# Turned row tiles of the hybrid layer: whole-row stores and 128-byte block loads for two of three token groups

## The chip, the cores and the metric

The kernel runs on one core of one Trainium2 chip. The metric is the device time of one execution in microseconds, the median over several runs. The engines are named as in the profile: PE is TensorE, DVE is VectorE, ACT is ScalarE, POOL is GpSimd, and SP is SyncE, which only issues DMAs. ScalarE's own DMA queue is shown as ACTq, SyncE's as SPq.

## The reference, cut to what matters

One layer for 2048 prompt rows and 128 sample rows of width 1024 (17 tiles of 128 rows). The first half mixes tokens (a gated delta rule in four heads beside a short gated convolution), and ends in the projection `w_o`. The change touches what comes then:

```python
mix = jnp.concatenate([o, sc_out.astype(x.dtype)], axis=-1) @ w_o
x = x + rmsnorm(mix, norm_mix_post)

h = rmsnorm(x, norm_ffn_pre)
f = (jax.nn.silu(h @ w_gate) * (h @ w_up)) @ w_down
x = x + rmsnorm(f, norm_ffn_post)
```

`w_gate` and `w_up` are 1024 x 2816, `w_down` is 2816 x 1024, all in float32.

## The kernel before, in words

**Stages.** Five groups of row tiles go through the mixing stage. Then the output stage takes the 17 row tiles one after the other (`o_tile`), and gate and up work on three token groups (`FGROUPS`) of tiles 0 to 5, 6 to 11 and 12 to 16. For each group 22 blocks `f` of 128 feed-forward columns are computed, each with seven products of a Strassen-like scheme (`product`, line 1436, 12 matmuls each since every factor is split into a high and a low part). The down projection follows.

**One output tile.** `o_load` brings the tile's mixed rows (`mr`, one buffer, two DMAs) and its rows of x (`xo`, two buffers). `mix_split` makes the high part `mh` on ScalarE (line 1154) and the low part `ml` on VectorE (line 1155). 48 matmuls (line 1198) fill two PSUM banks. ScalarE squares them (line 1202), VectorE scales them and adds them to `xo` (lines 1207 and 1208), ScalarE's queue stores the sum (`x2d`, line 1209). `o_rows` then makes the input of gate and up: squares on ScalarE (line 1217), a power on GpSimd, a scaling `hx` (line 1221) and a turn `ht` on VectorE (line 1223), which transposes each 32x32 block in place. `ht` has one buffer, so the turn of the next tile waits until the stores of this one have read it.

**The turned tile in DRAM.** Gate and up need columns of features on partitions, that is, the whole transpose. The 32x32 blocks are turned inside, and DMAs put them in their places. Before the change the store does that: `hTd` of a group is `[1024, rows of the group]`, and four DMAs a tile on SP's queue (line 1227) write 32 partitions each in runs of 32 floats, 128 bytes. `ffn_load` (line 1315) then reads eight tiles `fh` of 128 features in whole rows. ScalarE multiplies them by the gain (`ffn_gain`, line 1320), VectorE makes sums of them (`ffn_sums`), and `ffn_prep` splits them for the products.

**Order.** The first seven output tiles run alone. The eighth (`O_SPLIT`) and the next six have the preparation of token group one woven between them, and blocks 0 of gate and up begin among the last tiles. Weights of group one are loaded (`rg`, `ru`, lines 1399 and 1400), cast and split on ScalarE, VectorE and GpSimd into `fw` (lines 1411 and 1412), and some of the split weights are stored (`fsplit`, line 1414), which groups two and three load again (line 1409). Twelve slots hold split weights, a block uses seven. While group one is in gate and up, group two's `fh` tiles are loaded, one a block from f = 4, and multiplied and summed; the same for group three during group two. The instructions of every engine, and the DMAs of a queue, run in the order in which a planner at build time has put them: it simulates the engines with its own costs and takes, of the instructions that are ready, the one that comes first in the program. `tc.issue_after(x)` holds an instruction behind x on x's engine.

Of the kernel before, what the change touches and what calls it, by code (L numbers as in the profile page):

```python
# [9 lines left out]
F32 = mybir.dt.float32  # L10
# [7 lines left out]
P = 128  # L18
# [79 lines left out]
def kernel(  # L98
# [30 lines left out]
    mixo = [dram.tile([P, H, P], F32, name=f"mixo{t}") for t in range(NT)]  # L129
    mixs = [dram.tile([P, 4, len(g) * P], F32, name=f"mixs{gi}") for gi, g in enumerate(GROUPS)]  # L130
    wsplit = [dram.tile([P, 2, KD, P], F32, name=f"wsplit{j}") for j in range(28)]
    hTd = [dram.tile([D, len(g) * P], F32, name=f"hTd{gi}") for gi, g in enumerate(FGROUPS)]
    partd = [[dram.tile([len(g) // 2, P, 7, len(c) // 2, P], F32, name=f"partd{gi}_{ch}") for ch, c in enumerate(FCHUNKS)]
             for gi, g in enumerate(FGROUPS)]
    lastd = [dram.tile([P, 2, len(c) // 2, P], F32, name=f"lastd{ch}") for ch, c in enumerate(FCHUNKS)]
# [30 lines left out]
    with ExitStack() as ph:  # L166
# [1005 lines left out]
        def o_load(t):  # L1172
            mr = None
            if t:
                m = oa.tile([P, KD, P], F32, tag="mr", name="mr") if t > 1 else spare[2]
                mr = m[:, 0:4], m[:, 4:8]
                nc.sync.dma_start(out=mr[0], in_=mixo[t])
                gi, i = PLACE[t]
                nc.sync.dma_start(out=mr[1], in_=mixs[gi][:, :, i * P:(i + 1) * P])
            xt = op.tile([P, D], F32, tag="xo", name="xo", bufs=2)  # L1180
            nc.sync.dma_start(out=xt, in_=x[t])
            return mr, xt

        rows_in, omark = {0: o_load(0)}, {}

        def o_tile(t):
            mr, xt = rows_in.pop(t)
            halves_m = [mix_split(mr[kh]) if t else ready_m[kh] for kh in range(2)]
            if t + 1 < NT:
                rows_in[t + 1] = o_load(t + 1)  # L1190
            pss = [psd.tile([P, 512], F32, tag="d", name="dbank"), pft.tile([P, 512], F32, tag="t", name="ftbank")]
            for kh in range(2):
                mh, ml = halves_m[kh]
                for j in range(4):
                    k = 4 * kh + j
                    for ci, (m_, w_) in enumerate(((mh, woh), (mh, wol), (ml, woh))):
                        for n in range(2):
                            T.matmul(pss[n], m_[:, j, :], w_[k][:, n * 512:(n + 1) * 512],
                                     start=(k == 0 and ci == 0), stop=(k == KD - 1 and ci == 2))
            ss = op.tile([P, 4], F32, tag="oss", name="oss", bufs=2)  # L1200
            for n in range(2):
                A.activation(ojunk, pss[n], AF.Square, accum_out=ss[:, n:n + 1])
            V.tensor_add(ss[:, 0:1], ss[:, 0:1], ss[:, 1:2])
            r = rstd(op, ss[:, 0:1], 1, 1.0 / D, EPS, "ox")
            for n in range(2):
                c = slice(n * 512, (n + 1) * 512)
                V.scalar_tensor_tensor(pss[n], pss[n], r, gpost[:, c], op0=ALU.mult, op1=ALU.mult)
                omark["V"] = V.tensor_add(xt[:, c], xt[:, c], pss[n])  # L1208
            nc.scalar.dma_start(out=x2d[t], in_=xt)
            if t + 1 < NT:  # L1210
                o_rows(t, xt, ss)
            else:
                omark["last"] = lambda: o_rows(t, xt, ss)

        def o_rows(t, xt, ss):
            for n in range(2):
                omark["A"] = A.activation(ojunk, xt[:, n * 512:(n + 1) * 512], AF.Square, accum_out=ss[:, 2 + n:3 + n])
            V.tensor_add(ss[:, 2:3], ss[:, 2:3], ss[:, 3:4])
            r = rstd(op, ss[:, 2:3], 1, 1.0 / D, EPS, "oy")
            hx = op.tile([P, D], F32, tag="hx", name="hx") if t else spare[0]  # L1220
            V.tensor_scalar_mul(hx, xt, r)
            ht = op.tile([P, D], F32, tag="ht", name="ht") if t else spare[1]
            V.transpose(ht, hx)
            gi, i = FPLACE[t]
            for b in range(4):
                c = i * P + 32 * b
                nc.sync.dma_start(out=hTd[gi][:, c:c + 32].rearrange("(j f) c -> f j c", f=32),  # L1227
                                    in_=ht[32 * b:32 * b + 32].rearrange("f (j c) -> f j c", c=32))
# [12 lines left out]

    dring, dprep, cast, wl = {}, [], [], []
    SUMS = ("sA", "sB", "sC", "sD")
    SUMF = range(12, 20, 2)

    def down_chunk(ch):
        c = len(FCHUNKS[ch]) // 2
# [59 lines left out]
    with ExitStack() as ph:  # L1307
        ks = ctx.enter_context(tc.tile_pool(name="ks", bufs=1, reuse_waits="tile"))
        fp = ph.enter_context(tc.tile_pool(name="fp", bufs=1, reuse_waits="tile"))

        def ffn_load(gi, fs):
            hw = len(FGROUPS[gi]) * P // 2
            for k in range(KD):
                h = fs.tile([P, 2 * HW], F32, tag="h", name="fh", bufs=KD)
                nc.sync.dma_start(out=h[:, :2 * hw], in_=hTd[gi][k * P:(k + 1) * P])
                yield h[:, :2 * hw]

        def ffn_gain(hs, ks):
            for k in ks:
# [41 lines left out]
                yield X  # L1361

        with tc.tile_pool(name="fs", bufs=1, reuse_waits="tile") as fs:
            hload = ffn_load(0, fs)
            hs = [next(hload) for _ in range(KH)]
            o_tile(O_SPLIT)
            hs += hload
            prep = ffn_prep(0, hs, fs=fs)
            for i in range(len(PARTS)):
                with tc.issue_after(omark["A"].ins), tc.issue_after(omark["V"].ins):  # L1370
                    if i < 2:
                        ffn_gain(hs, range(KH * i, KH * i + KH))
                    hid = next(prep)
                if i + 1 < len(PARTS):
                    o_tile(O_SPLIT + 1 + i)
        fe = ph.enter_context(tc.tile_pool(name="fe", bufs=1, reuse_waits="tile"))

        nw = [0]
# [142 lines left out]
        for gi in range(len(FGROUPS)):  # L1521
            if gi:
                *_, hid = ffn_prep(gi, hs, t3)
            for f in range(NF):
                gate_up(gi, f, hid, gu_start(gi, f, hid))
                if (gi, f) == (0, 0):
                    omark["last"]()
                    ps_o.close()
                    fd = side.enter_context(tc.tile_pool(name="fd", bufs=1, reuse_waits="tile", side="right"))
                if f == 3 and gi + 1 < len(FGROUPS):  # L1530
                    hload, hs = ffn_load(gi + 1, fd), []
                if gi + 1 < len(FGROUPS):
                    if 5 <= f < 5 + KD:
                        with tc.issue_after(gmark["A"].ins):
                            ffn_gain(hs, [f - 5])
                    if 4 <= f < 4 + KD:
                        with tc.issue_after(wl[0].ins):
                            hs.append(next(hload))
                    if f in SUMF:
                        with tc.issue_after(gmark["V"].ins):  # L1540
                            t3 = ffn_sums(gi + 1, hs, fd, t3 if f > SUMF[0] else None, [SUMF.index(f)])
                elif f == 2:
                    side.close()
                    dr = late.enter_context(tc.tile_pool(name="dr", bufs=1, reuse_waits="tile", side="right"))
                    c = len(FCHUNKS[0]) // 2
                    a = dr.tile([P, 2, c * P], F32, tag="ar0", name="ar0")
                    with tc.issue_after(wl[0].ins):
                        nc.sync.dma_start(out=a, in_=partd[0][0][0, :, 0:2].rearrange("p i q c -> p i (q c)"))
                    first_parts = [dr.tile([P, 2, c * P], F32R, name=f"as0{i}") for i in range(3)]
                elif f == 4:  # L1550
                    with tc.issue_after(gmark["A"].ins), tc.issue_after(gmark["V"].ins):
                        for i, b in enumerate(first_parts[:2]):
                            A.copy(b[:, 0], a[:, i])
                            V.tensor_sub(b[:, 1], a[:, i], b[:, 0].bitcast(F32))
                    a = dr.tile([P, 2, c * P], F32, tag="ar0", name="ar0")
                    with tc.issue_after(wl[0].ins):
                        nc.sync.dma_start(out=a[:, 0], in_=partd[0][0][1, :, 0].rearrange("p q c -> p (q c)"))
                    dprep += [down_chunk(ch) for ch in dorder]
                    prep_step(1)
                elif f == 7:  # L1560
                    with tc.issue_after(gmark["A"].ins), tc.issue_after(gmark["V"].ins):
                        b = first_parts[2]
                        A.copy(b[:, 0], a[:, 0])
                        V.tensor_sub(b[:, 1], a[:, 0], b[:, 0].bitcast(F32))
                    prep_step(1)
                elif 10 <= f < 12 + NDR:
                    with tc.issue_after(gmark["A"].ins), tc.issue_after(gmark["V"].ins):
                        prep_step(1)
# [341 lines left out]
```

## Time and profile before

| | |
|---|---|
| time, median of 3 runs | 2432.32 us (2431.96 to 2433.75) |
| time of the profiled execution | 2432.03 us |
| its span | 2430.1 us |
| granted TensorE clock, mean | 0.998 |
| TensorE busy | 2406.1 us (99%) |
| VectorE, ScalarE, GpSimd busy | 1610.4, 1065.5, 560.5 us |
| output tiles and gate and up | from about 850 to 1967 us |
| DMA packets | 317464, of which 95700 under 512 bytes |

The span is the profiled execution from its first to its last instruction. A row of a timeline has the start, the duration, the engine and line, and in brackets the idle time before it with what ended it. A row of stretches has the busy time in each, the number of instructions, the granted clock (1.00 is full speed), the mean busy share of the 16 DMA engines and the GB/s they moved.

### The profile page before, as it was taken

Reading aid. Unit: us, or ns where it says so; the run is one execution under the profiler, and the core shown is the slowest. Engines: PE = TensorE matmul, PEld = TensorE weight load, DVE = VectorE, ACT = ScalarE, POOL = GpSimd, SP = SyncE. Lnnn points to the kernel's source line nnn. Section 1 sums busy time; section 2 is a strip of 40 time slices with the busy share of each in tenths; the row PEclk is TensorE's granted clock in tenths of the full one; section 3 lists DMA queues with packets and bytes.
Section 4 is the critical chain, followed back from the end, with each engine's and each line's share of the span. In section 5 each row is a group of like instructions: output and inputs, shape, how many; then the busy total and the mean of one; then the engine's idle time right before and its main releaser. Section 6 shows DMA issues by size and latency. Waiting matters only on the chain.

```text
span 2430.1 us, 39106 instructions
## 1 busy us (share of the span) xinstructions
PE 2406.1 (99%) x14222; PEld 2207.8 (91%) x14222; DVE 1610.4 (66%) x3042; ACT 1065.5 (44%) x2367; POOL 560.5 (23%) x667
## 2 busy tenths in 40 slices
PE   9999999999999999989999999999999999999998
PEld 7888889999999987889999999999999988888887
DVE  7875755746667465788888844456556555676787
ACT  6645545546444444444443423334333345333443
POOL 1211000001110000155665200000000035455663
PEclk9999999999999999999999999999999999999999
DMA  8774555666776677699877888878998844334376
GB/s 294 251 244 168 220 204 191 251 218 233 269 258 248 226 186 215 168 311 326 302 274 255 288 263 266 257 244 271 303 300 284 262 152 122 108 121 127 112 243 202
DMA packets 317464, 561.37 MB, mean 231 GB/s; under 512 B 95700, under 2 KB 198296, under 8 KB 299992
## 3 DMA queue, kind: packets, MB, share of 16 engines
q1 hardware_dynamic: 218848, 496.42, 61.7%
q10 hardware_dynamic: 98200, 61.41, 8.2%
q8 instruction: 112, 1.84, 0.3%
q0 software_dynamic: 224, 1.05, 0.1%
q14 instruction: 80, 0.66, 0.1%
HBM read 400.09 MB, written 158.70 MB: 230 GB/s over the span
## 4 chain that ended last, share of the span: by engine, by line
PE 51%; DMA 2%; DVE 2%; POOL 1%; issue 1%; SPq 1%; ACT 1%; ACTq 0%; POOLq 0%; DVEq 0%
PE fbank L1436 34%; PE fbank L1626 17%; DMA fsplit<-fw 1%; DMA partd<-pt 1%; SPq L1227 1%; POOL dw L1280 0%; DVE fw L1412 0%; DMA mr<-mixo 0%; DMA ru<-in_w_gu 0%; POOL as L1609 0%; DMA hTd<-ht 0%; ACTq L1473 0%; ACT as L1606 0%; DMA ar<-partd 0%; DMA xo<-in_x 0%
## 5 line engine op out<-in xcount | busy, mean ns | idle before, releaser
L1436 PE MATMUL fbank<-xh,fw 128*128 128x384 f32 (+1 forms) x3696 | 899.1, 326 | 8.4 <-DVE xo L1208 4.0
L1436 PEld LDWEIGHTS fbank<-xh,fw 128*128 128x128 f32 x3696 | 652.2, 188 | 10.8 <-ACT m L1469 3.9
L326 PE MATMUL dbank<-hi,w 128*128 128x384 f32 (+1 forms) x2224 | 650.6, 363 | 0.0
L1436 PE MATMUL fbank<-xl,fw 128*128 128x384 f32 (+1 forms) x1848 | 602.6, 326 | 0.0
L326 PEld LDWEIGHTS dbank<-hi,w 128*128 128x128 f32 x2224 | 409.7, 188 | 40.2 <-issue 3.6
L1626 PE MATMUL fbank<-dw,as 128*128 128x512 f32 x1785 | 415.9, 391 | 1.8 <-DVE as L1609 0.9
L1626 PEld LDWEIGHTS fbank<-dw,as 128*128 128x128 f32 x1785 | 334.6, 188 | 76.0 <-DVE as L1609 1.4
L326 PE MATMUL dbank<-lo,w 128*128 128x384 f32 (+1 forms) x1112 | 396.5, 357 | 0.0
L1436 PEld LDWEIGHTS fbank<-xl,fw 128*128 128x128 f32 x1848 | 347.3, 188 | 0.0
L326 PEld LDWEIGHTS dbank<-lo,w 128*128 128x128 f32 x1112 | 209.3, 188 | 15.7 <-DVE lo L241 0.4
L1609 POOL TENSOR_TENSOR as<-ar,as 128x256 fp32r<-128x256 f32 (+1 forms) x202 | 174.8, 874 | 182.3 <-ACT as L1606 176.7
L1606 ACT CAST as<-ar 128x256 fp32r<-128x256 f32 (+1 forms) x287 | 119.2, 427 | 206.5 <-PE fbank L1626 162.9
L1579 DVE TENSOR_TENSOR acc<-acc,fbank 128x512 f32<-128x512 f32 x219 | 148.1, 683 | 88.2 <-PE fbank L1626 70.8
L1280 POOL TENSOR_TENSOR dw<-dr,dw 128x512 fp32r<-128x512 f32 x48 | 67.8, 1422 | 512.5 <-ACT dw L1278 512.1
L1411 ACT CAST fw<-rg 128x512 fp32r<-128x512 f32 x124 | 77.2, 622 | 233.4 <-PE fbank L1436 140.3
L330 DVE SCALAR_TENSOR_TENSOR acc<-R,vec,acc 128x512 f32<-128x512 f32 (+2 forms) x180 | 120.9, 673 | 27.3 <-ACT acc L367 21.0
L1484 DVE TENSOR_TENSOR c<-u,fbank 128x384 f32<-128x384 f32 (+1 forms) x66 | 34.9, 528 | 94.4 <-PE fbank L1436 94.4
L1480 DVE TENSOR_TENSOR m<-m,m 128x384 f32<-128x384 f32 (+1 forms) x44 | 23.1, 526 | 83.1 <-ACT m L1470 82.9
L1412 POOL TENSOR_TENSOR fw<-rg,fw 128x512 fp32r<-128x512 f32 x44 | 65.5, 1489 | 35.9 <-ACT fw L1411 35.5
L1482 ACT ACTIVATE m<-fbank 128x384 f32<-128x384 f32 (+1 forms) x66 | 31.2, 473 | 90.9 <-PE fbank L1436 75.4
L359 POOL COPY hist<-R 128x3 f32<-128x3 f32 x60 | 18.3, 305 | 217.4 <-ACT R L335 171.9
L1487 ACT ACTIVATE c<-c 128x384 f32<-128x384 f32 (+1 forms) x66 | 33.4, 506 | 79.6 <-DVE c L1486 76.8
(402 smaller groups left out, 3566.6 us busy)
## 6 DMA issues: line engine op xcount, KB each, us to landing
w<-wsplit SPq DMA_DIRECT2D x105, 1024.0 KB, 5.0
fw<-fsplit SPq DMA_DIRECT2D x188, 512.0 KB, 4.7
fsplit<-fw SPq DMA_DIRECT2D x94, 512.0 KB, 4.0
partd<-pt ACTq DMA_DIRECT2D x86, 384.0 KB, 6.2
rg<-in_w_gu SPq DMA_DIRECT2D x62, 512.0 KB, 4.1
wsplit<-w SPq DMA_DIRECT2D x28, 1024.0 KB, 5.0
ar<-partd SPq DMA_DIRECT2D x43, 384.0 KB, 3.1
wr<-in_w_in SPq DMA_DIRECT2D x32, 512.0 KB, 6.5
```

What stands on the lines that cost most here:

```text
L326: T.matmul(ps[:, :c], l[:, k, :], r[k][:, :c], start=(k == 0 and r is hi and l is wh), stop=(k == KD - 1 and l is wl))
L330: r = V.scalar_tensor_tensor(acc, raw(d), w[:, d:d + 1], acc, op0=ALU.mult, op1=ALU.add)
L1280: e.tensor_tensor(out=w[1], in0=v, in1=w[0].bitcast(F32), op=ALU.subtract)
L1411: A.copy(w[:, 0], v)
L1412: e.tensor_tensor(out=w[:, 1], in0=v, in1=w[:, 0].bitcast(F32), op=ALU.subtract)
L1436: T.matmul(ps, w_[:, c], b_[k][:, :hw], start=(first and k == 0 and ci == 0), stop=(k == KH - 1 and ci == 2), skip_group_check=not first)
L1484: V.tensor_add(c21, u2, b3)
L1487: gmark["A"] = A.activation(c12, c12, AF.Silu)
L1579: mark_d["V"] = V.tensor_tensor(out=dst if out is None else out, in0=dst, in1=ps, op=ALU.add)
L1606: ins = mark_d["A"] = A.copy(a[:, 0, :n], v)
L1609: mark_d["V" if e is V else "G"] = e.tensor_tensor(out=a[:, 1, :n], in0=v, in1=a[:, 0, :n].bitcast(F32), op=ALU.subtract)
L1626: ins = T.matmul(ps, a[:, x_, q * P:(q + 1) * P], w[y_], start=(start and q == 0 and ci == 0), stop=(q == c - 1 and ci == 2), skip_group_c ...
```

## The change

Token group one stays as it was in DRAM. For groups two and three (tiles 6 to 16), `hTd` becomes `[4 x tiles, 32, 1024]`, and a turned tile is stored as it stands, one DMA of 128 whole rows of 4096 bytes, on ScalarE's queue. Placing the blocks moves to the load: each `fh` tile is filled by four DMAs on SP's queue, each of 32 partitions, which read runs of 128 bytes (24 runs a partition for group two, 20 for group three). There are 32 such loads a group, two a block from f = 4 to 15 and four in blocks 16 and 17 (`LOADF`), in the order of feature tiles 0, 4, 1, 5, 2, 6, 3, 7; a gain follows in the block after its tile's last load. The sums move from blocks 12, 14, 16, 18 to 12, 14, 17, 19 (`SUMF`). The eight loads of group one go into `o_tile` of tiles 7 and 8, four each, behind the row loads of the next tile.

```diff
-    hTd = [dram.tile([D, len(g) * P], F32, name=f"hTd{gi}") for gi, g in enumerate(FGROUPS)]
+    hTd = [dram.tile([4 * len(g), 32, D] if gi else [D, len(g) * P], F32, name=f"hTd{gi}") for gi, g in enumerate(FGROUPS)]
...
-        def o_tile(t):
+        def o_tile(t, loads=()):
...
             if t + 1 < NT:
                 rows_in[t + 1] = o_load(t + 1)
+            for load in loads:
+                load()
...
-            for b in range(4):
+            if gi:
+                nc.scalar.dma_start(out=hTd[gi][4 * i:4 * i + 4].rearrange("b f c -> (b f) c"), in_=ht)
+            for b in range(0 if gi else 4):
                 c = i * P + 32 * b
                 nc.sync.dma_start(out=hTd[gi][:, c:c + 32].rearrange("(j f) c -> f j c", f=32),
                                     in_=ht[32 * b:32 * b + 32].rearrange("f (j c) -> f j c", c=32))
...
-    SUMF = range(12, 20, 2)
+    SUMF = (12, 14, 17, 19)
+    LOADF = [4 + i // 2 for i in range(24)] + [16 + i // 4 for i in range(8)]
...
+        def ffn_tile(gi, fs):
+            return fs.tile([P, 2 * HW], F32, tag="h", name="fh", bufs=KD)[:, :len(FGROUPS[gi]) * P]
+
-        def ffn_load(gi, fs):
-            hw = len(FGROUPS[gi]) * P // 2
-            for k in range(KD):
-                h = fs.tile([P, 2 * HW], F32, tag="h", name="fh", bufs=KD)
-                nc.sync.dma_start(out=h[:, :2 * hw], in_=hTd[gi][k * P:(k + 1) * P])
-                yield h[:, :2 * hw]
+        def ffn_load(gi, fs, hs):
+            for k in (k for q in range(KH) for k in (q, KH + q)):
+                hs[k] = ffn_tile(gi, fs)
+                for q in range(4):
+                    c = k * P + 32 * q
+                    with tc.issue_after(wl[0].ins):
+                        nc.sync.dma_start(out=hs[k][32 * q:32 * q + 32].rearrange("f (b c) -> f b c", c=32),
+                                          in_=hTd[gi][:, :, c:c + 32].rearrange("b f c -> f b c"))
+                    yield k if q == 3 else None
...
-            hload = ffn_load(0, fs)
-            hs = [next(hload) for _ in range(KH)]
-            o_tile(O_SPLIT)
-            hs += hload
+            hs = [ffn_tile(0, fs) for k in range(KD)]
+            loads = [lambda k=k: nc.sync.dma_start(out=hs[k], in_=hTd[0][k * P:(k + 1) * P]) for k in range(KD)]
+            o_tile(O_SPLIT, loads[:KH])
...
-                    o_tile(O_SPLIT + 1 + i)
+                    o_tile(O_SPLIT + 1 + i, () if i else loads[KH:])
...
-                if f == 3 and gi + 1 < len(FGROUPS):
-                    hload, hs = ffn_load(gi + 1, fd), []
+                if f == 0 and gi + 1 < len(FGROUPS):
+                    hs = {}
+                    hload, loaded = ffn_load(gi + 1, fd, hs), []
                 if gi + 1 < len(FGROUPS):
-                    if 5 <= f < 5 + KD:
-                        with tc.issue_after(gmark["A"].ins):
-                            ffn_gain(hs, [f - 5])
-                    if 4 <= f < 4 + KD:
-                        with tc.issue_after(wl[0].ins):
-                            hs.append(next(hload))
+                    with tc.issue_after(gmark["A"].ins):
+                        while loaded:
+                            ffn_gain(hs, [loaded.pop()])
+                    for _ in range(LOADF.count(f)):
+                        k = next(hload)
+                        loaded += [] if k is None else [k]
```

## The prediction

> **What bounds the kernel now.** I read the page first, then TensorE's waits, then its busy time by stretches, then the timelines around each hole. From the page:
>
> ```profile
> span 2430.1 us, 39106 instructions
> PE 2406.1 (99%) x14222; PEld 2207.8 (91%) x14222; DVE 1610.4 (66%) x3042; ACT 1065.5 (44%) x2367; POOL 560.5 (23%) x667
> L1436 PE MATMUL fbank<-xh,fw 128*128 128x384 f32 (+1 forms) x3696 | 899.1, 326 | 8.4 <-DVE xo L1208 4.0 <-ACT m L1469 3.1 <-ACT m L1470 0.7
> ```
>
> TensorE is busy for all but 24 us, so the change can only win back holes in TensorE, and the slow clock behind a hole. It removes no matmul. Two places in reach of the change have holes: one before 960 us, and the start of gate and up from 1040 us, where line 1436 idles 8.4 us in all. Stretches of 10 us (busy time, matmuls, granted clock, DMA share, GB/s), then three longer ones over that start:
>
> ```profile
> 950.00:960.00 10.00, 7.33 (x26) 0.83 0.65 129
> ...
> 980.00:990.00 10.00, 10.00 (x46) 1.00 0.71 158
> ...
> 1050.00:1060.00 10.00, 9.65 (x46) 0.83 0.99 238
> ```
> ```profile
> 1040.00:1068.00 28.00, 23.66 (x119) 0.94 1.01 300
> 1068.00:1090.00 22.00, 19.29 (x110) 1.00 1.00 340
> 1090.00:1136.00 46.00, 44.81 (x257) 1.00 0.99 352
> ```
>
> The first hole costs more than its idle time. 26 matmuls ran where an undisturbed stretch runs 46, so (46-26)/46 x 10 = 4.3 us are lost: 2.67 idle, the rest at the lower clock. The second place loses 96 - 87.76 = 8.2 us of idle time and (1-0.83) x 10 = 1.7 us of clock, 9.9 together, and the DMA engines are saturated throughout. So 4.3 + 9.9 = 14.2 us is the most that lies here.
>
> **The first hole** is a wait for the store that the change moves. Start, duration, and the idle time before it with what ended it, on SP's queue, ScalarE, VectorE and TensorE:
>
> ```profile
> 933.87 4.77 SPq L1315 DMA_DIRECT2D fh<-hTd  x8
> ...
> 941.72 6.24 SPq L1227 DMA_DIRECT2D hTd<-ht  x4
> ```
> ```profile
> 949.99 1.12 ACT L1154 CAST mh<-mr 128x512 fp32r<-128x512 f32 x2
> ```
> ```profile
> 937.24 1.25 DVE L1223 STREAM_TRANSPOSE ht<-hx 128x1024 f32<-128x1024 f32 x1
> ...
> 947.88 0.75 DVE L1221 TENSOR_SCALAR hx<-xo,oyr 128x1024 f32<-128x1024 f32 x1 [0.73 <-POOL oyr L155]
> 952.64 1.25 DVE L1223 STREAM_TRANSPOSE ht<-hx 128x1024 f32<-128x1024 f32 x1 [4.00 <-DMA hTd<-ht]
> 953.80 1.25 DVE L1155 TENSOR_TENSOR ml<-mr,mh 128x512 fp32r<-128x512 f32 x2
> ```
> ```profile
> 954.51 0.79 PE L1198 MATMUL dbank<-woh,ml 128*128 128x512 f32 x1 [2.67 <-DVE ml L1155]
> ```
>
> Tile 6 is turned by 938.5, but SP is busy with eight loads and with the next tile's rows, and starts the four stores at 941.72. There is one buffer ht, so the turn of tile 7, whose input was ready at 948.6, waits until 952.64. Behind it on VectorE stands ml, for which TensorE waits.
>
> **Part 1, eleven turned tiles (6 to 16) stored in whole rows on ScalarE's queue.** Removed are 44 DMAs on SP, added 11 on ScalarE. Prices: two short stretches, the first filled with the old stores and the second with loads in long rows; then issue times (minimum/median/maximum, ns), and from the page an issue with its us to landing:
>
> ```profile
> 897.60:899.80 2.20, 2.20 (x11) 1.00 1.11 171
> 938.00:940.00 2.00, 2.00 (x10) 1.00 1.02 410
> ```
> ```profile
> L1227 SPq DMA_DIRECT2D hTd<-ht x68: 303/564/3530, 873.3 to 1082.4; - x68
> ...
> L1209 ACTq DMA_DIRECT2D x2d<-xo x17: 326/327/333, 869.1 to 1062.9; - x17
> ```
> ```profile
> x2d<-xo ACTq DMA_DIRECT2D x17, 512.0 KB, 2.6
> ```
>
> The x2d store has the size, shape and queue of the new one: 0.33 us to issue, 2.6 to land. Tile 6 would be issued at about 938.6 and landed by 942, six us ahead of tile 7's input. The turn then runs 948.6 to 949.9, ml can start when the first mh is done (950.6) and ends near 951.3; TensorE ran dry at 951.8. The hole closes, by half a microsecond: **-4.3 us**.
>
> The Trainium skill, "DMA: Bandwidth & Descriptors", section Issuing engines are not separate DMA queues, says that another issuing engine saves only the sequencer's issue time, usually small beside the transfer. By that alone this move would be worth next to nothing and the time would stay at 2432. The first half fits the trace; the second doesn't, since SP's issues took 6.24 us for one tile, and they stood behind others.
>
> **Where it lies in the tail.** The last tiles' stores meet weight loads, split-weight stores and saturated engines; the last row below is the packets from 1040 to 1100 us:
>
> ```profile
> 1045.11 6.15 SPq L1227 DMA_DIRECT2D hTd<-ht  x4
> 1051.36 1.49 SPq L1399 DMA_DIRECT2D rg<-in_w_gu  x1
> ...
> 1075.49 8.29 SPq L1227 DMA_DIRECT2D hTd<-ht  x4
> ```
> ```profile
> 1054.52 1.25 DVE L1223 STREAM_TRANSPOSE ht<-hx 128x1024 f32<-128x1024 f32 x1 [3.07 <-DMA hTd<-ht]
> ```
> ```profile
> 1056.33 0.62 ACT L1411 CAST fw<-rg 128x512 fp32r<-128x512 f32 x1 [3.52 <-DMA rg<-in_w_gu]
> ```
> ```profile
> 1048.60 0.41 PE L1436 MATMUL fbank<-xh,fw 128*128 128x384 f32 x1 [3.37 <-DVE xo L1208]
> ```
> ```profile
> DMA packets 19267, 19.39 MB, mean 323 GB/s; under 512 B 14080, under 2 KB 15083, under 8 KB 19264
> ```
>
> These issues leave SP, so rg and ru go out earlier. A tile's 524,288 bytes take 3.1 us at 171 GB/s and 1.3 at 410: 1.8 us of the engines freed a tile, and at 4096 short packets a tile the 14080 are 3.4 tiles: some 6 us freed in a stretch that is full. Of the 8.4 us idle on line 1436, 4.0 are two waits for xo. The 3.37 at 1048.60 falls before the 3.07 wait for ht and hangs on VectorE's order; I leave it and its 1.7 us of clock where they are. The other, 0.6, comes behind the 3.07 wait and goes. The remaining 4.4 are ScalarE's copies and casts, late through weights and slots held by transfers; I take three quarters, 3.3, since six freed microseconds exceed them but queueing is not additive. Bounds: nothing, or all 9.9. Taken: **-3.9 us**.
>
> **The new wait.** ScalarE now waits for VectorE's turn of each tile; the squares, mh casts, weight casts and copies out of PSUM stand behind it, and TensorE waits for those. In the steady part ScalarE has idle time there:
>
> ```profile
> ACT mh L1154 <- PE ftbank L1198: 19.8, 5, 4.0
> ```
>
> Tile 6's turn ends at 938.5 and that idle time spans it, so the issue and the wait cost nothing; without this cover it would be up to 4 us a tile before TensorE's next mh. In the tail the place in ScalarE's queue isn't visible from the trace of before. Bounds: 0, and 3.4 tiles, rounded up to four, x (1.25 for the turn + 0.33), about 6 us, less what it idles anyway (it waits 3.52 us for rg alone). I take 0, since ScalarE is the idle one there.
>
> **Part 2, loads of groups two and three.** 16 loads of whole rows become 64, each on 32 partitions in runs of 128 bytes: 768 runs (group two) or 640. Nothing in the trace reads runs of 128 bytes from DRAM. The nearest row below is the long-row rate, 410 GB/s (98,304 bytes: 0.24 us), the nearest above the old stores at 171 (0.57 us, or 12 ns a run on each engine), of equal run and partition count but the other way. I take the latter. Reads may be dearer; that end is a rival. Where they run, two a block f, four at f = 16 and 17:
>
> ```profile
> 1218.50:1246.00 27.50, 27.50 (x161) 27.50 (x160) 23.16 (x29) 13.60 (x26) 16.15 (x12) 1.00 0.78 263
> ...
> 1466.00:1493.50 27.50, 27.50 (x160) 27.50 (x159) 12.27 (x23) 8.40 (x17) 0.00 (x0) 1.00 0.87 282
> ```
> ```profile
> SPq L1409 <- PE fbank L1436: 141.9, 66, 3.6
> ```
>
> A block is 84 matmuls, 84 x 27.5/160 = 14.4 us. Two loads are 1.15 us of the engines where one load of 393,216 bytes took 0.96, so the DMA share of 0.78 to 0.87 rises by about 0.01, and TensorE has no hole there. SP spends 64 x 0.56 = 36 us on issues instead of the 44 removed; it waits 141.9 us for TensorE to free weight slots in the 300 us from 1390 on (the last row), which covers them. Cost: **0**. The work of the gains and of the sums is the same; they move by a block or two and end at f = 19 instead of 18, three blocks before their use.
>
> The Trainium skill, same page, section Why small descriptors are slow, gives about 3 cycles of overhead a packet: 128 bytes are 4 beats, so 4/7 of the page's 435 GB/s, an estimate of 249, 0.39 us a load. The store row is slower; with the page's rate the sum stays as it is.
>
> **Part 3, group one's eight loads behind the next tile's rows.** Same bytes. At 933.87 all eight went ahead of the next tile's row loads. Behind them, the rows can come earlier and the gains later, by at most half of those 4.77 us of issues. The first hole was closed above with the old order, so I take 0, with 2.4 us either way.
>
> **Sum.** The profiled execution took 2432.03 us, 0.3 under the median of 2432.32. 2432.0 - 4.3 - 3.9 = 2423.8; I forecast **2424**.
>
> **Rivals.**
> - *Only the first hole closes.* VectorE's order and the weight supply, not the stores, make the tail. For: the largest hole, 3.37 us, is before any wait for ht. Against: rg stands behind 6.15 us of store issues. 2432.0 - 4.3 = 2427.7.
> - *Everything closes*, since xo comes earlier too once row loads aren't late: 2432.0 - 14.2 = 2418. Against: that wait runs through VectorE, whose work there stays.
> - *ScalarE held in the tail* takes the place of the waits removed: -4.3, tail unchanged, + 6 = 2434. It decides if copies out of PSUM stand behind a turn that VectorE does late.
> - *Dear short reads: slower.* Place: group two, where group three's tiles are loaded. Room in a block is 0.13 x 14.4 = 1.9 us plus 0.8 of the old load (327,680 bytes), 2.7 in all, 1.35 a load, 40 runs on each engine: from 34 ns a run on, weights come late. At 40 ns a load takes 1.6: 0.5 us over in 12 blocks and 3.7 in two, 13 us, so 2424 + 13 = 2437, and beyond with a higher price. Against: 34 ns is nearly three times the store's 12.
> - *The change does less than it says*, because the planner that orders the queues shifts other work: 2432.
>
> **How the numbers follow.** A measurement of this kernel can tell about 0.2%, 4.9 us, from no change: faster is under 2427.5, slower over 2437.2. Forecast 0.40, everything 0.14, first hole alone 0.18 (half of it on each side of 2427.5), ScalarE held 0.12, less than it says 0.05, dear reads 0.11. Faster: 0.40 + 0.14 + 0.09 = 0.63. Slower: dear reads and 0.02 of ScalarE held, 0.13. Same: 0.24. The range leaves out most of the dear reads and the edges: 2416 to 2435; the forecast's own is 2420 to 2428.
>
> **What would show it.** Right: no idle time on VectorE's turn for hTd; TensorE full from 950 to 960 at clock 1.00; no store issue of turned tiles on SP after 930; under 8.2 us idle on line 1436; gate and up without a hole from 1140 to 1960, at a DMA share within a few hundredths; new loads issued in under 1 us and landing in 3 to 6. Wrong: holes of TensorE behind fw between 1150 and 1690 (dear reads), or ScalarE idle until ht with TensorE waiting for its copies.

## The result, and the profile after

The changed kernel takes 2420.8 us (median of six, 2419.26 to 2423.34), the kernel before 2433.29 beside it (2431.96 to 2437.0): a ratio of 0.9948, 95% interval 0.9935 to 0.9961. It is faster, by 12.5 us by the medians. The profiled execution took 2421.49 us, its span is 10.6 us shorter than before's (2430.1 to 2419.5).

From the page of the changed kernel, where lines from 1198 on have moved down by two (1200 is the former 1198) and those of gate and up by ten (1446 is the former 1436, 1479 the former 1469); in the experiments they move by a few more:

```profile
span 2419.5 us, 39078 instructions
PE 2402.4 (99%) x14222; PEld 2204.9 (91%) x14222; DVE 1603.4 (66%) x3042; ACT 1064.3 (44%) x2367; POOL 561.3 (23%) x667
L1446 PE MATMUL fbank<-xh,fw 128*128 128x384 f32 (+1 forms) x3696 | 898.2, 326 | 2.7 <-ACT m L1479 1.7
```

TensorE's idle time fell from 24.0 us (2430.1 - 2406.1) to 17.1 (2419.5 - 2402.4), that is by 6.9; its busy time fell by 3.7, with the same matmuls, mostly because the two stretches of 10 us at a granted clock of 0.83 are gone (1.7 us each). Together 10.6, the difference of the two profiled spans; the 12.5 above are between medians of other executions, and a later measurement gives 10.5 (below). The two places, by TensorE's busy time, first in the kernel before (the line of 1040 to 1136 was summed in the prediction), then after (columns: busy us, matmuls, granted clock, DMA share, GB/s):

```profile
1040.00:1136.00 96.00, 87.76 (x482) 0.98 1.00 334
```
```profile
950.00:960.00 10.00, 10.00 (x45) 1.00 0.62 197
1040.00:1136.00 96.00, 94.29 (x543) 1.00 0.93 324
```

The first hole is closed. The start of gate and up has 1.7 us of idle time left of 8.2, and none of the lower clock.

The turned tiles' stores and the new loads in the changed kernel (issue time minimum/median/maximum in ns, first and last start, and, last line, from issue to landing of the loads), and two rows of ScalarE and its queue:

```profile
L1228 ACTq DMA_DIRECT2D hTd<-ht x11: 326/326/327, 942.2 to 1061.9; - x11
```
```profile
L1325 SPq DMA_DIRECT2D fh<-hTd x64: 422/498/3179, 1081.1 to 1617.9; - x64
...
DMA to landing us min/median/max: 4.1/4.6/9.2
```
```profile
942.20 0.33 ACTq L1228 DMA_DIRECT2D hTd<-ht  x1
```
```profile
942.63 0.60 ACT L1204 ACTIVATE ojunk<-dbank 128x512 bf16<-128x512 f32 x1 [6.79 <-DMA fh<-hTd]
```

A store takes 0.33 us to issue, as forecast. But tile 6's left at 942.20, not at 938.6, and ScalarE stood 6.79 us before its next piece of work. TensorE didn't notice. The move to another queue didn't bring this store forward: before it left at 941.72, with short runs on ScalarE's queue (first experiment) at 941.48, with whole rows on SP's at 941.86. What ScalarE stood for, when the turn was done at about 939.0, isn't settled: the profile names the landing of group one's loads.

**Where the time came from** shows in ScalarE's rows of the output tiles. Before, the first mh casts of tiles 15 and 16 and the first squares of tiles 13 to 16:

```profile
1017.14 0.62 ACT L1154 CAST mh<-mr 128x512 fp32r<-128x512 f32 x1 [3.43 <-DMA mr<-mixo]
1018.08 0.59 ACT L1202 ACTIVATE ojunk<-dbank 128x512 bf16<-128x512 f32 x1
...
1030.94 0.62 ACT L1154 CAST mh<-mr 128x512 fp32r<-128x512 f32 x1 [2.89 <-DMA mr<-mixo]
1031.47 0.59 ACT L1202 ACTIVATE ojunk<-dbank 128x512 bf16<-128x512 f32 x1
...
1040.13 0.59 ACT L1202 ACTIVATE ojunk<-dbank 128x512 bf16<-128x512 f32 x1
...
1049.62 0.60 ACT L1202 ACTIVATE ojunk<-dbank 128x512 bf16<-128x512 f32 x1
```

And after:

```profile
1011.27 0.62 ACT L1154 CAST mh<-mr 128x512 fp32r<-128x512 f32 x1 [2.90 <-PE ftbank L1200]
...
1022.24 0.62 ACT L1154 CAST mh<-mr 128x512 fp32r<-128x512 f32 x1 [2.86 <-PE ftbank L1200]
1027.96 0.60 ACT L1204 ACTIVATE ojunk<-dbank 128x512 bf16<-128x512 f32 x1 [0.39 <-PE dbank L1200]
...
1038.94 0.60 ACT L1204 ACTIVATE ojunk<-dbank 128x512 bf16<-128x512 f32 x1 [2.00 <-PE dbank L1200]
```

Before, ScalarE waits for the rows of the next tile (mr), and the squares of tiles 13 and 14, which TensorE has already finished, stand behind that cast. Tile 15's squares (1040.13) stand behind casts of the first split weights instead. VectorE's rows, first before and then after, show the sum that these casts wait for and tile 15's xo, for which TensorE waited 3.37 us:

```profile
1037.77 1.19 DVE L1402 TENSOR_TENSOR sC<-rg,ru 128x512 f32<-128x512 f32 x1 [0.17 <-DMA ru<-in_w_gu]
...
1047.18 0.68 DVE L1208 TENSOR_TENSOR xo<-xo,dbank 128x512 f32<-128x512 f32 x1
```
```profile
1025.63 0.69 DVE L1412 TENSOR_TENSOR sC<-rg,ru 128x512 f32<-128x512 f32 x1 [0.67 <-DMA ru<-in_w_gu]
...
1034.54 0.68 DVE L1210 TENSOR_TENSOR xo<-xo,dbank 128x512 f32<-128x512 f32 x1
```

After, ScalarE's casts and squares above wait for TensorE. The last tile's squares start 10.7 us earlier (1049.62 to 1038.94), tile 15's xo 12.6. SP's queue says where the rows and the weights were held, before and after:

```profile
1021.33 3.59 SPq L1227 DMA_DIRECT2D hTd<-ht  x4
1025.03 0.60 SPq L1177 DMA_DIRECT2D mr<-mixo  x1
...
1031.69 0.38 SPq L1399 DMA_DIRECT2D rg<-in_w_gu  x1
```
```profile
1013.61 0.32 SPq L1177 DMA_DIRECT2D mr<-mixo  x1
...
1019.07 0.33 SPq L1409 DMA_DIRECT2D rg<-in_w_gu  x1
```

The store of one tile holds SP for 3.59 us and the next rows go out right behind it. After the change the last rows (of tile 16) go out 11.4 us earlier, the first gate weights 12.6. That is a loop: late rows, late squares, late xo and turn, late store, and so the next late rows. Whether SP's issue time drives it, or the time of the short runs on the DMA engines, is what the experiments ask.

### The profile page after: what moved, and what is told of

Its sections match the earlier page's. It is cut to its first block, busy times and chain, and to the rows that moved or that the text cites. A ratio compares the mean times of both kernels' runs of the same rounds, so it can differ in the third digit from the quotient of the medians.

```text
span 2419.5 us, 39078 instructions
## 1 busy us (share of the span) xinstructions
PE 2402.4 (99%) x14222; PEld 2204.9 (91%) x14222; DVE 1603.4 (66%) x3042; ACT 1064.3 (44%) x2367; POOL 561.3 (23%) x667
## 4 chain that ended last, share of the span: by engine, by line
PE 93%; DVE 3%; ACT 1%; DMA 1%; POOL 1%; issue 1%; POOLq 0%; SPq 0%; DVEq 0%; ACTq 0%
PE fbank L1446 36%; PE dbank L326 25%; PE fbank L1637 17%; PE dbank L1200 4%; PE ftbank L1200 4%; PE tbank L384 1%; PE gbank L597 1%; PE gbank L604 1%; PE obank L776 1%; PE gbank L768 1%; PE gbank L790 1%; PE obank L798 1%; PE gbank L784 1%; DVE sA L1413 0%; PE gbank L701 0%
```

## The experiments

**The queue alone.** The kernel before, with the four short-run stores of tiles 6 to 16 on ScalarE's queue.

```diff
-                nc.sync.dma_start(out=hTd[gi][:, c:c + 32]...
+                (nc.scalar if gi else nc.sync).dma_start(out=hTd[gi][:, c:c + 32]...
```

> The kernel before with one edit: the four block stores of tiles 6 to 16 are issued on ScalarE's queue instead of SyncE's; layout, runs of 128 bytes and loads stay old. Theory Q (what counts is that the stores leave SyncE's queue, where they stood behind loads and held weight loads up): the wait of the turn for the store before tile 7 goes, the hole near 955 us closes (-4.3 us), and part of the tail's 9.9 us goes too, less what ScalarE now loses by issuing four stores a tile among its copies: ratio to before 0.9955 to 0.9980. Theory L (what counts is the short runs): the first hole closes, the tail stays full of short packets and ScalarE is held by slow issues: 0.998 to 1.003.

Measured: 2441.14 us, ratio 1.0036 (1.0023 to 1.0048): slower. ScalarE and its queue:

```profile
941.48 6.86 ACTq L1227 DMA_DIRECT2D hTd<-ht  x4
```
```profile
948.44 0.60 ACT L1202 ACTIVATE ojunk<-dbank 128x512 bf16<-128x512 f32 x1 [13.00 <-DMA hTd<-ht]
...
1057.14 7.21 ACTq L1227 DMA_DIRECT2D hTd<-ht  x4
1064.39 0.48 ACT L1469 COPY m<-fbank 128x384 f32<-128x384 f32 x1 [7.21 <-DMA hTd<-ht]
```

The four issues hold ScalarE as long as they held SP (6.24 us before), and its squares stand behind them, at the end of 13 us in which ScalarE does no work. The first hole stays (7.56 us busy from 950 to 960), although both theories had it closed, and the tail is worse (84.90 us busy from 1040 to 1136, where it was 87.76): TensorE waits 3.78 us for the copy in the last row. The queue doesn't make an issue cheaper here; it only chooses who is held.

**The layout alone.** The changed kernel with the whole-row stores back on SP's queue.

```diff
-                nc.scalar.dma_start(out=hTd[gi][4 * i:4 * i + 4]..., in_=ht)
+                nc.sync.dma_start(out=hTd[gi][4 * i:4 * i + 4]..., in_=ht)
```

> The changed kernel with one edit: the whole-row store of a turned tile is issued on SyncE's queue. Theory L (one store of long rows instead of four of short runs is what counts): the issue takes about 0.4 us instead of 2.6 to 8.3 a tile, the buffer of the turn comes free in time, and the time is within 2 us of the changed kernel: ratio to before 0.994 to 0.996. Theory Q (the queue counts): the store stands behind group one's loads and the row loads again, the hole near 955 us is back: 0.997 to 0.999.

Measured: 2419.63 us, ratio 0.9945 (0.9932 to 0.9959): the whole gain without ScalarE's queue. Later this kernel ran beside the changed one on one chip:

> The changed kernel once more, beside the next run on one chip, to compare the two queues directly. If ScalarE's queue for the whole-row stores were worth something of its own (ScalarE held by a store costs, or SP relieved by it gains): the two ratios lie apart by 0.002 or more. If, as the runs so far suggest, only the length of the rows counts: both at 0.994 to 0.996 and within 0.001 of each other.

> The changed kernel with the whole-row stores on SP's queue instead of ScalarE's (e2 once more, beside the run above). ScalarE's queue matters: apart from the run above by 0.002 or more. Only the length of the rows matters: 0.994 to 0.996, within 0.001 of it.

Measured: the changed kernel 2421.29 us (2420.56 to 2423.22), ratio 0.9961 (0.9949 to 0.9974); with the stores on SP 2419.22 us (2418.04 to 2420.24), ratio 0.9951 (0.9938 to 0.9965). They lie 0.001 apart, at the border of the second expectation, and the single times don't overlap: SP's queue is some 2 us better, if anything. It is the fastest kernel of this study. Two rows of ScalarE in it show that the stand of 6.79 us is gone:

```profile
939.46 0.60 ACT L1204 ACTIVATE ojunk<-dbank 128x512 bf16<-128x512 f32 x1 [4.29 <-PE dbank L1200]
944.11 0.62 ACT L1154 CAST mh<-mr 128x512 fp32r<-128x512 f32 x1 [3.25 <-DMA mr<-mixo]
```

**Group one's order alone.** The kernel before, with its eight loads of group one behind the next tile's rows (Part 3).

```diff
-            hload = ffn_load(0, fs)
-            hs = [next(hload) for _ in range(KH)]
-            o_tile(O_SPLIT)
-            hs += hload
+            o_tile(O_SPLIT, loads[:KH])
```

> The kernel before with one edit: only the eight loads of group one are moved behind the next tiles' row loads; stores and loads of groups two and three stay old. Prediction: nothing, within 2.4 us: ratio 0.999 to 1.001. Rival O (the order of these loads closes the first hole, since the row loads and the stores of tile 6 no longer stand behind eight loads): 0.998 or less, the hole near 955 us gone.

Measured: 2434.87 us, ratio 1.0008 (1.0000 to 1.0017). TensorE's stretches:

```profile
950.00:960.00 10.00, 10.00 (x46) 1.00 0.97 200
1040.00:1136.00 96.00, 84.41 (x461) 0.96 0.96 314
```

The first hole is closed, with the short stores still on SP and VectorE still waiting 7.0 us for them. It is worth nothing: the tail loses 96 - 84.41 = 11.6 us of idle time and 3.8 of clock where it lost 8.2 and 1.7, so 5.5 us are given back.

**Group one's order undone.** The changed kernel with those loads where they were.

> The changed kernel with one edit: the eight loads of group one go back to their old places. Prediction: as the changed kernel, ratio to before 0.994 to 0.996. Rival O: the first hole comes back, 0.9965 or more.

Measured: 2422.64 us, ratio 0.9959 (0.9946 to 0.9971), about 1.8 us over the changed kernel, inside both intervals. The two orders can't be told apart by the time. Half of the first hole's idle time is back, none of its lower clock, and the tail is that of the changed kernel (94.29 us busy from 1040 to 1136), so the gain there doesn't need the order:

```profile
950.00:960.00 10.00, 8.68 (x39) 1.00 0.57 199
```

**SP's issue time or the DMA engines' time.** Two kernels made from the one with whole rows on SP: each tile stored three times, and each tile stored in sixteen pieces.

```diff
                 nc.sync.dma_start(out=hTd[gi][4 * i:4 * i + 4]..., in_=ht)
+                for n in range(2):
+                    nc.sync.dma_start(out=spareh[2 * t + n], in_=ht)
```
```diff
-                nc.sync.dma_start(out=hTd[gi][4 * i:4 * i + 4]..., in_=ht)
+                for n in range(0, P, 8):
+                    nc.sync.dma_start(out=rows[n:n + 8], in_=ht[n:n + 8])
```

> The kernel with whole rows stored from SP's queue (e2), but each of the eleven turned tiles is stored three times, the second and third time into spare DRAM. Three long-row stores put about 3 x 1.28 = 3.8 us a tile on the DMA engines (1.28 us: 524,288 bytes at 410 GB/s), more than the 3.07 us of the old short-run store (at 171 GB/s), but hold SP for only three issues of some 0.33 us, 1.0 us a tile, against 2.6 to 6.2 before. Theory S (the gain comes from SP's issue time: the rows of the next tile are issued earlier): ratio 0.994 to 0.9965, nearly e2's 0.9945, TensorE idle from 1040 to 1136 us under 4 us. Theory E (the gain comes from the time on the DMA engines): the whole gain is lost, ratio 0.998 to 1.002, and TensorE idles some 8 us from 1040 to 1136 us.

> The other half of the same question: whole rows stored from SP's queue, in sixteen DMAs of 8 partitions each instead of one of 128. The bytes and the long rows are those of e2, about 1.3 us of the DMA engines a tile, but SP is held for sixteen issues of some 0.33 us, 5.2 us a tile, as long as with the old short-run stores (2.6 to 6.2). Theory S (SP's issue time): most of the gain is lost, ratio 0.998 to 1.001, ScalarE waits 2 to 4 us for the rows (mr) of tiles 13 and 14 as before, and the squares of tile 16 start near 1049 us again. Theory E (time on the DMA engines): as e2, ratio 0.994 to 0.996, squares of tile 16 near 1039.

Measured: three times 2424.04 us, ratio 0.9964 (0.9951 to 0.9976); in sixteen issues 2433.62 us, ratio 1.0004 (0.9996 to 1.0013). Sixteen issues of the same bytes in the same long rows take the whole gain away; tripled bytes, with more time on the DMA engines than the old stores by the estimate above, take away about a third of it (some 4 us), and part of that is SP again, held for 1.2 to 2.7 us a tile. So SP's issue time is the main cause, and the engines' time is worth at most 4 us.

The two doses aren't equal, though: the sixteen issues hold SP for 5.9 to 10.95 us a tile, 90 us in all, not the 5.2 a tile that were expected, and the old stores of these tiles held it for 47. That SP's hold at its old size costs the whole gain isn't shown. Nor do these runs show how evenly a piece of 8 partitions spreads over the engines; if all of them went to half of the engines, those would be busy 2.6 us a tile (twice 1.28, an estimate), less than with tripled bytes.

The sixteen issues on SP, and what stood behind them:

```profile
1024.44 10.95 SPq L1230 DMA_DIRECT2D hTd<-ht  x16
...
1053.58 9.80 SPq L1230 DMA_DIRECT2D hTd<-ht  x16
1063.42 0.36 SPq L1411 DMA_DIRECT2D rg<-in_w_gu  x1
```
```profile
1029.96 0.62 ACT L1154 CAST mh<-mr 128x512 fp32r<-128x512 f32 x1 [4.25 <-DMA mr<-mixs]
...
1041.82 0.60 ACT L1204 ACTIVATE ojunk<-dbank 128x512 bf16<-128x512 f32 x1
...
1058.75 0.62 ACT L1423 CAST fw<-rg 128x512 fp32r<-128x512 f32 x1 [4.28 <-DMA rg<-in_w_gu]
```

One step of the expectation failed: the last tile's squares start at 1041.82, not near 1049. Nonetheless the time is that of before, since in the tail the same queue holds the gate and up weights. TensorE idles 11.8 us from 1040 to 1136 (84.22 busy), and it waits for copies of ScalarE (3.2 + 0.6), for casts and splits of weights (2.5 on ScalarE, 2.0 on VectorE, 1.2 on GpSimd) and for xo (2.1). So rows and weights are both late behind a held SP, and the 10.7 us of the squares aren't the one measure of the gain.

**Which tiles count.** The changed kernel with whole rows for one token group only.

```diff
-    hTd = [dram.tile([4 * len(g), 32, D] if gi else [D, len(g) * P], ...
+    hTd = [dram.tile([4 * len(g), 32, D] if gi == 1 else [D, len(g) * P], ...
```

> The changed kernel, but whole rows (and the short loads in gate and up) for token group two alone, tiles 6 to 11; tiles 12 to 16 go back to four short-run stores on SP's queue. Theory T (what counts are the stores that stand in SP's queue ahead of the last tiles' rows and the first weights, from 1000 us on; before that a late row is absorbed, as the closed first hole of e3 was): no gain, ratio 0.998 to 1.001, TensorE idle 8 to 12 us from 1040 to 1136 us. Theory A (every tile's store costs its own share): 6 of 11 tiles, ratio near 0.9975.

> The other half: whole rows and short loads for token group three alone, tiles 12 to 16, the stores of tiles 6 to 11 as four short-run DMAs on SP's queue. Theory T (the last tiles' stores count): nearly the whole gain, ratio 0.995 to 0.997, TensorE idle under 4 us from 1040 to 1136 us. Theory A (every tile's store costs its own share): 5 of 11 tiles, ratio near 0.998.

Measured: tiles 6 to 11 alone 2425.91 us, ratio 0.9973 (0.9963 to 0.9983); tiles 12 to 16 alone (`gi == 2`) 2429.57 us, ratio 0.9990 (0.9981 to 0.9999). Theory T, that only the last tiles' stores count, falls, by the second run above all. Theory A has the first value and nearly the second. TensorE's stretch, first for tiles 6 to 11, then for 12 to 16, and the last tile's squares in the latter:

```profile
1040.00:1136.00 96.00, 91.13 (x511) 0.98 0.97 314
```
```profile
1040.00:1136.00 96.00, 89.60 (x510) 1.00 0.91 329
```
```profile
1043.74 0.60 ACT L1204 ACTIVATE ojunk<-dbank 128x512 bf16<-128x512 f32 x1
```

Lateness that the earlier tiles pile up is carried into the tail: with short runs for tiles 6 to 11 the last squares are still 4.8 us late (1043.74 against 1038.94), though TensorE has no hole before 1040. The two gains add up to 0.0037, of 0.0039 to 0.0052 for both.

**The short reads.** First the same bytes in whole rows, 8 loads a group (the blocks of groups two and three aren't placed, so that this kernel leaves out part of the data movement that the result needs), then short loads four times as dense.

```diff
+                    nc.sync.dma_start(out=hs[k], in_=rows[k])
-                        nc.sync.dma_start(out=hs[k][32 * q:32 * q + 32]..., in_=hTd[gi][:, :, c:c + 32]...)
```
```diff
-    LOADF = [4 + i // 2 for i in range(24)] + [16 + i // 4 for i in range(8)]
+    LOADF = [4 + i // 8 for i in range(32)]
```

> The changed kernel, but the loads of groups two and three in gate and up take the same bytes in whole rows, 8 DMAs a group instead of 32 of 128-byte runs. This leaves out the placing of the 32x32 blocks, so the outputs of those two groups aren't the reference's; the time of every other operation is kept. My prediction priced the short reads at 12 ns a run on each engine (0.57 us a load, hidden): the time is that of the changed kernel, ratio 0.994 to 0.996, and the DMA share from 1150 to 1690 us falls by about 0.01. If the short reads cost something that is hidden only in part: 0.991 to 0.993.

> The changed kernel, with the loads of 128-byte runs four times as dense: eight in each of the blocks f = 4 to 7 instead of two in most of f = 4 to 15 and four in 16 and 17. At 12 ns a run a load takes 0.57 us of the engines, a block 4.6 us, against 1.9 us of room and what the weights' slots buffer: TensorE loses nothing or up to 4 x 2.7 = 11 us over one group, less by the weights that are loaded ahead; ratio 0.9945 to 0.998. At 34 ns a run (the point at which my rival of dear short reads begins) a block needs 10 to 13 us: 30 us and more are lost in each of the two groups, ratio above 1.01.

Measured: long reads 2423.61 us, ratio 0.9963 (0.9950 to 0.9975), so no gain over short ones; dense reads 2425.67 us, ratio 0.9970 (0.9960 to 0.9981). All engines from 1136 to 1690 us, in which nearly all loads run (the last two numbers are DMA share and GB/s), in the changed kernel and with long reads:

```profile
1136.00:1690.00 554.00, 553.02 (x3190) 551.19 (x3189) 358.71 (x554) 210.94 (x422) 123.95 (x89) 1.00 0.85 267
```
```profile
1136.00:1690.00 554.00, 551.93 (x3183) 550.24 (x3182) 359.44 (x554) 210.55 (x421) 124.33 (x89) 1.00 0.81 267
```

The short runs cost 0.04 x 554 = 22 us of the engines' time. Eight of the 64 loads start before this stretch. With the 12.1 us that the 4.98 MB of the other 56 take in long rows (at 410 GB/s) that is 34 us, or 0.61 us for each, of 695 runs in the mean, 43 on each of 16 engines: an estimate of 14 ns a run (12 to 16 by the rounding of the shares). TensorE loses nothing by it. Of the dense reads only the first group's start hurts, where the engines are full (DMA share 0.98 from 1040 to 1136). TensorE's hole, ScalarE and its queue, and SP's queue:

```profile
1126.65 0.69 PE L1446 MATMUL fbank<-xh,fw 128*128 128x384 f32 x1 [4.97 <-ACT m L1478]
```
```profile
1111.85 7.57 ACTq L1483 DMA_DIRECT2D partd<-pt  x3
1119.46 0.62 ACT L1421 CAST fw<-rg 128x512 fp32r<-128x512 f32 x1 [11.64 <-DMA partd<-pt]
```
```profile
1100.99 7.41 SPq L1325 DMA_DIRECT2D fh<-hTd  x6
...
1117.22 8.10 SPq L1325 DMA_DIRECT2D fh<-hTd  x6
```

There a load took 1.2 to 1.35 us to issue, and SP was held again. But ScalarE's queue was held too: three stores of partial sums took 7.57 us to issue, where three at the same place take 2.08 in the changed kernel (at 1110.56), and the work of ScalarE, for which TensorE waits, stood behind them. From 1136 to 1690 TensorE was busy for all of 554.0 us, the second dense group included.

## Why the prediction was right, step by step

The forecast, faster by 8.2 us at 2424, had the sign, and the time is inside its range. The steps fared less evenly: one term was too small, and one that came out as forecast did so in part for another reason.

- **First hole, -4.3.** It closed, but not by the stated way alone. The rows that come ahead of group one's loads close it without any change to the store, and the whole-row store without that order closes half (1.32 us idle are left of 2.67). I had put the order at 0. In the changed kernel VectorE's ml comes first and the turn of tile 7 later than I had it (948.6), without a wait (VectorE's rows):

```profile
948.51 0.69 DVE L1155 TENSOR_TENSOR ml<-mr,mh 128x512 fp32r<-128x512 f32 x1 [0.16 <-ACT mh L1154]
951.38 1.25 DVE L1225 STREAM_TRANSPOSE ht<-hx 128x1024 f32<-128x1024 f32 x1
```

  By itself the closed hole is worth nothing, since the tail gives it back. The profile showed that a wait would go; it didn't show that the next place would take the time.
- **Tail, -3.9.** This is the term that was mis-sized. 6.5 us of idle time and all 1.7 of clock came back, 8.2 of 9.9. I left the wait of 3.37 for xo at 1048.60 alone because it falls before VectorE's wait for ht and hangs on VectorE's order. That order is the same after, but all of it comes 12 us earlier. The wait hung on tile 15's squares on ScalarE, those on weight casts, and these on the weights and on tile 14's xo, whose squares stood behind mh; weights and mh's rows went out late behind SP's issues of earlier tiles. One wait was followed one step back; more steps led to the store. The two steps sum to 12.5, near the rival in which everything closes (2418), whose reason, rows that are no longer late, was the right one. That the sum equals the medians' 12.5 is chance: the profiled spans are 10.6 apart, mainly because TensorE idles 0.8 us more from 1136 to 1690 and 0.7 more before 860, which the change doesn't touch.
- **Engines freed in the tail, six microseconds.** Not the main cause: with more time on the engines two thirds of the gain stay, and sixteen issues lose all of it. The first reason of the same paragraph, that rg and ru go out earlier, is the one that holds.
- **ScalarE's queue.** Its issue time was right (0.33 us). The date of tile 6's store was 3.6 us off, and the assumption that ScalarE has time to wait held: a stand of 6.79 us cost TensorE no hole. As the reason for the gain the move to this queue falls. I held the Trainium skill's rule (DMA: Bandwidth & Descriptors, section Issuing engines are not separate DMA queues) to be contradicted by the trace. For the queue it was right: with whole rows the two queues give 2421.3 and 2419.2 us. Only its remark that the issue is usually small doesn't hold for the old stores, 6.24 us for a tile.
- **ScalarE held in the tail** didn't decide in the changed kernel; with short runs on its queue it did (ratio 1.0036, and 7.21 us in which a copy stood behind four issues).
- **Short reads, 12 ns a run, cost 0.** Confirmed: 14 ns, nothing lost, and the rival from 34 ns falls. The estimate worked out from the Trainium skill (DMA: Bandwidth & Descriptors, section Why small descriptors are slow), 0.39 us a load of 768 runs, is below what came out here (0.61 for 695). The rise of the DMA share was 0.04 (0.81 to 0.85 in the stretch above), not 0.01: I set two new loads against one old in one block, but the old loads stood in eight blocks (f = 4 to 11), the new ones stand in fourteen, and the last two of these have four each.

## What to carry to other kernels

In this kernel a DMA in many short runs cost the queue that issues it first, and every load behind it in program order; look at the start-to-start times on that queue, and count issue time as work of that engine. Change the layout so that the issue is one short one before choosing a queue: the queue only decides whose work is held. And follow a wait back until its chain reaches a queue or TensorE itself; a hole that closes is a gain only if the next place doesn't wait for something else.

## What the runs showed that I had not expected

- The time to issue a DMA isn't fixed. One of 1,024 short runs took 0.56 us in the median and up to 3.53; four of them in the saturated tail 8.29. A long-row DMA of 512 KB took 0.33. Eight partitions of it, a sixteenth of the bytes, took 0.29 in the median, but sixteen in a row 10.95, 0.68 each, at the worst place. ScalarE starts no work of its own behind such an issue (6.86 us for four), as SP starts no other DMA.
- Reads and writes of 128-byte runs cost about the same on the engines here: about 14 ns a run by the difference of two kernels, 12 by the old stores' rate.
- With denser loads on SP's queue, three stores of partial sums on ScalarE's took 7.57 us to issue instead of 2.08, and TensorE lost 4.97 us behind them.
- ScalarE can stand for 6.8 us at one place without a matmul lost, and a late row that makes no hole before 1040 still costs 5 us after it (idle from 1040 to 1136: 6.4 us with short runs for tiles 6 to 11, 1.4 with whole rows for all on SP).
